# Eight smallest experts in two shared tiles of four instead of four shared tiles of two, with weights loaded in the order in which they are used

## The chip, the cores and the metric

The kernel runs on one core of one Trainium2 chip. The metric is device time in microseconds (us) of one launch. Three runs of the kernel before took 1531.68, 1537.52 and 1541.69 us; the median is 1537.52 us.

The engines are named as the profile names them: PE multiplies matrices (PEld is its weight load), DVE, ACT and POOL work on vectors, SP issues transfers. A line number such as L1372 is a line of the kernel before, unless the text says that it is of the changed kernel.

## The reference

One layer of a model on a sequence of 1024 tokens of 1024 values: a recurrent mixer with two branches, then a mixture of 32 experts in 4 groups of 8. The change touches only the mixture. What it computes:

```python
def hier_moe(h, w_rg, b_rg, w_re, b_re, w1e, w3e, w2e):
    t = h.reshape(-1, d)
    pg_top, g_idx = lax.top_k(softmax(t @ w_rg + b_rg), 1)          # one group of 4
    le_sel = (t @ w_re + b_re) of that group                        # its 8 experts
    pe_top, e_idx = lax.top_k(softmax(le_sel), TOP_K)               # TOP_K = 2
    wts = pg_top * pe_top / sum(pe_top)
    ...
    for e in range(N_EXPERTS):                                      # 32
        he = silu(t @ w1e[e]) * (t @ w3e[e])                        # 1024 -> 256
        out = out + cw[:, e:e + 1] * (he @ w2e[e])                  # 256 -> 1024
```

Each token is worked on by two experts, so there are 2048 rows of expert work in all. How many rows an expert gets comes from the data. With the reference's own inputs experts 0, 1 and 2 get 55, 19 and 15 rows, and the other 29, sorted by size, get 249, 197, 179, 137, 127, 88, 73, 73, 66, 64, 64, 61, 57, 53, 52, 51, 49, 47, 47, 38, 37, 29, 27, 22, 21, 16, 13, 11 and 11.

## The kernel before

The program is fixed when it is built, but which expert is large is known only on the chip. So there are **places**: experts 0 to 2 have places of their own (NF = 3) with 128 rows each, and the other 29 experts are sorted by size on the chip and take 29 places with a fixed number of rows, the classes CLS: 256, 224, 192 twice, 128 three times, 112, 96 three times, 80 twice and 64 sixteen times. A place of up to 128 rows is one tile of 128 partitions; a larger one is two tiles. Rows that do not fit into their place go to overflow tiles (NX = 16), which are worked on at the end, only where there are any. Two places of 64 rows are a **pair** and share one tile: partitions 0 to 63 hold the rows of the one, 64 to 127 those of the other.

The routing stage builds, for every tile, the list of the rows that belong on its partitions. 32 small matmuls (L1242) add up 0/1 matrices into `pi`, one column for each tile; the second member of a pair must land on partitions 64 to 127, so 32 more matmuls (L1245) with 64 columns add it there. Three DVE instructions make from `pi` the lists `sidx` (where a row of the result goes, L1249) and `gidx` (which token to fetch, L1250).

The expert stage is a list of **jobs**, one for each tile, worked on in order, each with its gather of 128 rows (POOL, L1289), transposes (PE, `turn` L1302, `turn2` L1362), `up` (1024 to 512 columns), `hidden` (L1324 to L1328), `down` (256 to 1024) and a scatter of the result (POOL, L1333). While a job's `up` runs the next job's rows are gathered, and its transposes stand behind that `up` on PE. The classes are interleaved: each class's units are spread evenly over the sequence. The jobs of the stage are, in order (S for a place of its own with its rows, x2 for two tiles, P for a pair):

```
before: S128 S128 S128 P S128 S96 P S192x2 S80 P P S256x2 S224x2 S128 S112 S96 P P S192x2 S80 P S128 S96 P
after:  S128 S128 S128 P S128 S96 S192x2 S80 Q P S256x2 S224x2 S128 S112 S96 P S192x2 S80 Q S128 S96 P
```

A single's weights are split into two parts that PE can multiply fast (`split`, ACT L1282 and DVE or POOL L1283, into 8 buffers each for `wh` and `wl`), and `up` and `down` do three such products for each step (L1315 to L1317, L1350 to L1352). A pair's weights are used as they are loaded, with one slower product for each step, and the two members' products go to different columns of PE's array (`up2` L1372, `down2` L1386):

```python
def up2(W, tp):
    ph = psum.tile([128, 512], F32, name="ph", bufs=2)
    for k in range(8):
        o = (k % 2) * 512
        for s_ in range(2):
            C = slice(64 * s_, 64 * s_ + 64)
            T.matmul(ph[C], tp[:, k, C], W[s_][k // 2][:, o:o + 512], start=(k == 0), stop=(k == 7))
```

An expert's weights are 6 **pieces** of 512 KB, c0 to c3 for `up` and c4 and c5 for `down`. All 192 pieces go through SP's one queue in a fixed order (L953) into NRAW = 16 buffers `w`; a piece's transfer waits until the piece 16 places before it has been used up, by its split (a single) or by PE (a pair). `issue` keeps the loads LA = 3 experts ahead in the program; what holds them back on the chip is the 16 buffers. Before the change the order is expert by expert, c0 to c5.

Of the kernel before, what the change touches and what calls it, by code (L numbers as in the profile page):

```python
# [21 lines left out]
LA = 3  # L22
# [70 lines left out]
def _build(tc, A, out, dump, stop, top):  # L93
    nc = tc.nc
    V, S, T, P, Y = nc.vector, nc.scalar, nc.tensor, nc.gpsimd, nc.sync
# [15 lines left out]
    psum = front.enter_context(pool("psum", 1, PSUM))  # L111
# [16 lines left out]
    ident = const.tile([128, 128], F32, name="ident")  # L128
# [61 lines left out]
    def derive(name, n):  # L190
# [5 lines left out]
                    op0=OP.mult, op1=OP.add)  # L196
# [521 lines left out]
    order = [(p, hf) for p in range(4) for hf in range(2)]  # L718
# [55 lines left out]
    psum = p3.enter_context(pool("psum3", 1, PSUM))  # L774
# [115 lines left out]
    iot = rpc.tile([128, 128], F32, name="iot")  # L890
# [18 lines left out]
    for d in range(8):  # L909
        merge(1, d)  # L910
        for kk in (2 * d, 2 * d + 1):
# [4 lines left out]
            h, l = (lambda t: (t[:, 0], t[:, 1]))(wo.tile([128, 2, 512], F32R, name="w", bufs=NRAW))  # L916
# [5 lines left out]
    if stop == "merged":  # L922
# [11 lines left out]
    NS = ND - 2 * NP  # L934
    NB = sum(c > 128 for c in CAP)

    NTP = NF + NB + NS
    NT0 = NTP + NP
    NT = NT0 + NX

    units = [[(p,) for p in range(sum(m for m, _ in CLS[:q]), sum(m for m, _ in CLS[:q + 1]))]
             for q in range(len(CLS) - 1)] + [[(NS + 2 * i, NS + 2 * i + 1) for i in range(NP)]]
    order = [p for _, u in sorted(((i + 0.5) / len(us), u) for us in units for i, u in enumerate(us)) for p in u]
    raws, src = {}, {}
    issued = [0]

# [9 lines left out]
    def issue(n):  # L956

        while issued[0] < min(n, 192):
            e, c = divmod(issued[0], 6)
            if c == 0:  # L960
# [57 lines left out]
    PO = [rp.tile([128, 2, 8, 128], BF, name=f"PO{i}") for i in range(2)]  # L1018
# [41 lines left out]
    with pool("xt", 1) as xt:  # L1060
# [78 lines left out]
    dmp("m_gt2", mrow["gt2"])  # L1139
    gidx = x1p.tile([128, NT], I32, name="gidx")  # L1140
    sidx = x1p.tile([128, NT], I32, name="sidx")
    ordi = x1p.tile([128, 32 + NX + 1], I32, name="ordi")
    with pool("psumr", 1, PSUM) as psum, pool("ro", 1, side="right") as ro:
        f = lambda shape, name, dt=F32, pl=rp: pl.tile(shape, dt, name=name)
# [8 lines left out]

        plan = f([32, 3, 32], "plan")
        for dst, base, step in ((plan[:, 0, 0:NB], NF, 2), (plan[:, 0, NB:NS], NF + 2 * NB, 1),
                                (plan[:, 0, NS:ND:2], NTP, 1), (plan[:, 0, NS + 1:ND:2], NT, 1),
                                (plan[:, 0, ND:32], 0, 1)):
# [32 lines left out]
        c = lambda i: cc[:, i:i + 1]  # L1190
# [37 lines left out]
        ts = f([128, 2, 8], "ts")  # L1228
# [7 lines left out]
        RT = f([128, 2, 8, NT + NP], "RT", BF, pl=ro)  # L1236
        bt = lambda ap: ap.to_broadcast([128, 2, 8, NT + NP])
        last = V.tensor_tensor(RT, bt(iot[:, None, None, 0:NT + NP]), bt(ts[:, :, :, None]), op=OP.is_equal)
        pi = psum.tile([128, NT], F32, name="pi")
        ajh = [(a, j, h) for a in range(2) for j in range(8) for h in range(2)]  # L1240
        for a, j, h in ajh:
            T.matmul(pi, PO[h][:, a, j], RT[:, a, j, 0:NT], start=((a, j, h) == ajh[0]), stop=False,  # L1242
                     skip_group_check=True)
        for a, j, h in ajh:
            T.matmul(pi[64:128, NTP:NT0], PO[h][:, a, j, 0:64], RT[:, a, j, NT:], start=False,  # L1245
                     stop=((a, j, h) == ajh[-1]), skip_group_check=True)
        li = f([128, NT], "li", pl=ro)
        V.tensor_scalar(li, pi, 0.0, 4096.0, op0=OP.is_equal, op1=OP.mult)
        V.scalar_tensor_tensor(sidx, pi, -1.0, li, op0=OP.add, op1=OP.add)  # L1249
        V.tensor_scalar(gidx, sidx, 1, None, op0=OP.arith_shift_right)  # L1250
# [23 lines left out]
    with pool("psume", 1, PSUM) as psum, pool("ew", 1) as ew, pool("ex", 2) as ex:  # L1274
# [19 lines left out]
        def turn(xg, m):  # L1294

            R = slice(0, m)
            th = ex.tile([128, 8, 128], F32R, name="th")
            tl = ex.tile([128, 8, 128], F32R, name="tl")
            for i in range(2):
                pt = psum.tile([128, 4, 128], F32, name="pt", bufs=3)  # L1300
                for k in range(4):
                    T.transpose(pt[:, k, R], xg[R, (4 * i + k) * 128:(4 * i + k) * 128 + 128], ident[R, R])  # L1302
# [51 lines left out]
            scatter(yt, ti, m)  # L1354


        def turn2(xg):
            tp = ex.tile([128, 8, 128], F32, name="th")
            for i in range(2):
                pt = psum.tile([128, 4, 128], F32, name="pt", bufs=3)  # L1360
                for k in range(4):
                    T.transpose(pt[:, k], xg[:, (4 * i + k) * 128:(4 * i + k) * 128 + 128], ident)  # L1362
                S.copy(tp[:, 4 * i:4 * i + 4], pt)  # L1363
            return tp

        def up2(W, tp):
            ph = psum.tile([128, 512], F32, name="ph", bufs=2)
            for k in range(8):
                o = (k % 2) * 512
                for s_ in range(2):  # L1370
                    C = slice(64 * s_, 64 * s_ + 64)
                    T.matmul(ph[C], tp[:, k, C], W[s_][k // 2][:, o:o + 512], start=(k == 0), stop=(k == 7))  # L1372
            return ph

        def down2(W, ph, ti):
            pt = hidden(ph, 128)
            ep = ex.tile([128, 2, 128], F32, name="eh")
            S.copy(ep, pt[:, 0:2])
            yt = ex.tile([128, 1024], F32, name="yt")
            for hf in range(2):  # L1380
                sl = slice(hf * 512, hf * 512 + 512)
                py_ = psum.tile([128, 512], F32, name="py", bufs=3)
                for k in range(2):
                    for s_ in range(2):
                        C = slice(64 * s_, 64 * s_ + 64)
                        T.matmul(py_[C], ep[:, k, C], W[s_][4 + k][:, sl], start=(k == 0), stop=(k == 1))  # L1386
# [3 lines left out]
        def tiles_of(p):  # L1390
            b = NF + p + min(p, NB)
            return [(b + i, min(128, CAP[p] - 128 * i)) for i in range(-(-CAP[p] // 128))]


        jobs = [((e,), e, 128) for e in range(NF)]
        for n, p in enumerate(order):
            if p < NS:
                jobs += [((NF + n,), t, m) for t, m in tiles_of(p)]
            elif (p - NS) % 2 == 0:
                jobs.append(((NF + n, NF + n + 1), NTP + (p - NS) // 2, 128))  # L1400
# [12 lines left out]

        def turned_of(n, xg):
            es, _, m = jobs[n]
            return turn2(xg) if len(es) == 2 else turn(xg, m)
# [4 lines left out]
        for n, (es, ti, m) in enumerate(jobs):  # L1421
            nxt = jobs[n + 1] if n + 1 < len(jobs) else None
            if nxt:
                xg = gather(n + 1, *nxt[1:])
            pair = len(es) == 2
# [68 lines left out]
```

## Time and profile before

| | |
|---|---|
| median of three runs | 1537.52 us |
| profiled execution | 1536.43 us |
| its span, first to last instruction | 1534.5 us |
| PE busy | 1326.4 us (86%), mean granted clock 0.945 |
| DVE, ACT, POOL busy | 920.1, 490.3, 408.1 us |
| expert stage: first transposes to last `down` on PE | 1137.1 to 1466.6 us |
| jobs in it: tiles of singles, pairs | 20, 8 |
| last piece of weights issued by SP | 1442.5 us |

How to read it: in the profile times are in us from the first instruction and "mean ns" is that of one instruction. PE's matmuls overlap, so the distance between starts tells what one costs, not its length. A slow product is two matmul instructions in the trace. A stage is judged by what its last engine waits for: PE for weights, or SP's queue for a buffer that PE still holds. "DMA share" is the part of the time in which the 16 transfer engines were busy, and GB/s what they moved.

### The profile page before, as it was taken

To read this page: it belongs to the slowest core of one execution; us is meant where nothing else is said; L and a number is where in the kernel's file an instruction comes from. 1 tells how busy PE (TensorE), PEld (TensorE's weight loads), DVE (VectorE), ACT (ScalarE), POOL (GpSimd) and SP (SyncE) were. 2 spreads that over 40 slices of the span, in tenths; PEclk is the share of its full clock that TensorE was granted. 3 is DMA by queue.
4 is the path that set the end of the run, shared out by engine and by line. 5 is a ranking of instruction groups with operands and counts; after the bars stand their busy time and mean duration, and the time that the engine had idled before them with its cause. 6 is when DMAs were issued, how large, how long until landed. Compare 5 with 4: busy or idle time off the path is not lost.

```text
span 1534.5 us, 23186 instructions
## 1 busy us (share of the span) xinstructions
PE 1326.4 (86%) x8524; PEld 926.5 (60%) x8524; DVE 920.1 (60%) x2073; ACT 490.3 (32%) x900; POOL 408.1 (27%) x327
## 2 busy tenths in 40 slices
PE   1898998899999999999999797899759899999910
PEld 0686765666766667766766475687545555755500
DVE  8936868687658562475433577614775435625557
ACT  3222323132222222231211693312424424514321
POOL 7001212121101110111111326601314434634514
PEclk9998999999999999999999899999969999999965
DMA  6333432333433211112211754541448979979952
GB/s 262 130 117 138 126 110 92 99 99 115 151 131 94 66 57 35 51 57 60 63 42 35 238 167 150 187 163 56 165 165 299 385 281 402 349 267 393 349 234 100
DMA packets 113403, 248.59 MB, mean 162 GB/s; under 512 B 39632, under 2 KB 40960, under 8 KB 112256
## 3 DMA queue, kind: packets, MB, share of 16 engines
q1 hardware_dynamic: 105952, 230.22, 42.7%
q0 software_dynamic: 7328, 16.79, 3.0%
q8 instruction: 69, 1.13, 0.3%
q14 instruction: 54, 0.44, 0.1%
HBM read 218.16 MB, written 38.36 MB: 167 GB/s over the span
## 4 chain that ended last, share of the span: by engine, by line
PE 60%; DVE 20%; DMA 9%; ACT 4%; issue 4%; POOL 2%; POOLq 0%; SPq 0%; DVEq 0%; ACTq 0%
PE pg L319 5%; PE pg L318 5%; PE pg L320 5%; DMA xg<-h2d,gidx 3%; DMA w<-in_we 3%; PE ph L1372 3%; PE pj L318 2%; DVE wa L228 2%; PE pj L320 2%; PE pj L319 2%; PE st L603 2%; PE ph L1315 2%; PE st L617 2%; PE pj L1106 2%; PE ph L1317 2%
## 5 line engine op out<-in xcount | busy, mean ns | idle before, releaser
L318 PE MATMUL pg<-hh,wh 128*128 128x512 f32 x376 | 158.9, 423 | 8.4 <-DVE cr L680 5.0
L319 PE MATMUL pg<-hl,wh 128*128 128x512 f32 x376 | 157.2, 418 | 0.0
L320 PE MATMUL pg<-hh,wl 128*128 128x512 f32 x376 | 155.9, 415 | 0.0
L560 POOL TENSOR_TENSOR WV<-VT,m 128x512 f32<-128x512 f32 x32 | 35.5, 1110 | 369.5 <-PE st L603 280.3
L1282 ACT CAST wh<-w 128x1024 fp32r<-128x1024 f32 x96 | 98.5, 1053 | 82.1 <-DMA w<-in_we 30.7
L1283 DVE TENSOR_TENSOR wl<-w,wh 128x1024 fp32r<-128x1024 f32 x68 | 92.0, 1376 | 36.1 <-ACT wh L1282 33.7
L228 DVE SCALAR_TENSOR_TENSOR wa<-wa,cb 128x1024 f32<-128x1024 f32 x64 | 79.6, 1251 | 27.1 <-DMA wa<-in_wada 27.0
L318 PEld LDWEIGHTS pg<-hh,wh 128*128 128x128 f32 x376 | 72.3, 192 | 33.3 <-issue 9.4
L216 ACT CAST wh<-wr 128x512 fp32r<-128x512 f32 x88 | 54.4, 619 | 100.0 <-PE pj L319 50.4
L217 DVE TENSOR_TENSOR wl<-wr,wh 128x512 fp32r<-128x512 f32 x72 | 53.5, 742 | 50.7 <-ACT wh L216 50.4
L319 PEld LDWEIGHTS pg<-hl,wh 128*128 128x128 f32 x376 | 72.3, 192 | 17.7 <-issue 4.7
L320 PEld LDWEIGHTS pg<-hh,wl 128*128 128x128 f32 x376 | 71.9, 191 | 17.2 <-issue 4.0
L610 DVE SCALAR_TENSOR_TENSOR St<-St,Dc,st 128x64 f32<-128x64 f32 x128 | 35.4, 277 | 76.4 <-PE st L608 76.3
L318 PE MATMUL pj<-hh,wh 128*128 128x512 f32 x192 | 77.5, 404 | 3.2 <-DVE carry L365 3.2
L1283 POOL TENSOR_TENSOR wl<-w,wh 128x1024 fp32r<-128x1024 f32 x28 | 71.0, 2541 | 30.6 <-ACT wh L1282 23.1
L320 PE MATMUL pj<-hh,wl 128*128 128x512 f32 x192 | 76.9, 401 | 0.0
L319 PE MATMUL pj<-hl,wh 128*128 128x512 f32 x192 | 75.8, 395 | 0.0
L1315 PE MATMUL ph<-wh,th 128*128 128x512 f32 (+4 forms) x160 | 65.4, 409 | 7.1 <-ACT th L1304 6.8
L515 DVE TENSOR_TENSOR X<-X,UC 128x60 f32<-128x60 f32 (+24 forms) x248 | 65.9, 266 | 4.2
L1372 PE MATMUL ph<-w,th 128*64 128x512 f32 x256 | 65.7, 598 | 1.8 <-ACT th L1363 1.7
L513 DVE TENSOR_TENSOR UC<-X,Ui 128x60 f32<-128x60 f32 (+24 forms) x248 | 63.3, 255 | 4.4
L1317 PE MATMUL ph<-wh,tl 128*128 128x512 f32 (+4 forms) x160 | 63.9, 399 | 1.9 <-DVE tl L1305 1.9
(503 smaller groups left out, 3139.0 us busy)
## 6 DMA issues: line engine op xcount, KB each, us to landing
w<-in_we SPq DMA_DIRECT2D x192, 512.0 KB
wa<-in_wada SPq DMA_DIRECT2D x64, 512.0 KB
wr<-in_win SPq DMA_DIRECT2D x72, 256.0 KB
gd<-gt SPq DMA_DIRECT2D x32, 256.0 KB
g<-gd SPq DMA_DIRECT2D x32, 256.0 KB
yy<-yd SPq DMA_DIRECT2D x8, 1024.0 KB
xT<-in_xT SPq DMA_DIRECT2D x8, 512.0 KB
Ui<-Ud SPq DMA_DIRECT2D x32, 128.0 KB
```

Source lines behind the costliest of these rows:

```text
L216: S.copy(h[:, :n], raw)
L228: V.scalar_tensor_tensor(wa, wa, 1.0, cb, op0=OP.mult, op1=OP.mult, accum_out=ccol[:, i:i + 1])
L318: T.matmul(ps, wh[:, o:o + 128], hh[k][:, sl], start=(k == 0), stop=False)
L319: T.matmul(ps, wh[:, o:o + 128], hl[k][:, sl], start=False, stop=False)
L320: T.matmul(ps, wl[:, o:o + 128], hh[k][:, sl], start=False, stop=(k == n - 1))
L513: V.tensor_mul(t_, X[:, :nj, s:s + 1].to_broadcast([128, nj, nt]), Ui[:, s, None, s + 1:32].to_broadcast([128, nj, nt]))
L515: V.tensor_add(X[:, :nj, s + 1:32], X[:, :nj, s + 1:32], t_)
L1282: S.copy(h, raw)
L1283: (P if pool_engine else V).tensor_sub(l, raw, h.bitcast(F32))
L1315: T.matmul(ph[R], th[:, k, R], h[:, o:o + 512], start=(k == 0), stop=False)
L1317: T.matmul(ph[R], tl[:, k, R], h[:, o:o + 512], start=False, stop=(k == 7))
L1372: T.matmul(ph[C], tp[:, k, C], W[s_][k // 2][:, o:o + 512], start=(k == 0), stop=(k == 7))
```

## The change

The 16 places of 64 rows become 8 places of 64 (4 pairs) and 8 places of 32, the smallest, in 2 tiles of four (Q, a **quad**): 26 jobs instead of 28. `up2` and `down2` loop over two or four members with 64 or 32 partitions each. The pieces of a shared tile are loaded c0 of every member, then c1 of every member, and so on. The sets of rows that a shared tile's later members need are no longer added by 32 matmuls: `pi` gets 10 extra columns, and after `sidx` and `gidx` of the single tiles are made, five small products with a shifted identity (`shf_`) move those columns to partitions 32, 64 or 96 and add them, and the lists of the shared tiles are made from that.

```diff
-    NF, NX, NP = 3, 16, 8
-    CLS = ((1, 256), (1, 224), (2, 192), (3, 128), (1, 112), (3, 96), (2, 80), (2 * NP, 64))
+    NF, NX, NP, NQ = 3, 16, 4, 2
+    CLS = ((1, 256), (1, 224), (2, 192), (3, 128), (1, 112), (3, 96), (2, 80), (2 * NP, 64), (4 * NQ, 32))
...
+    NG_ = NP + 3 * NQ
...
+    order, pieces, upto = [], [(e, c) for e in range(NF) for c in range(6)], {e: 6 * e + 6 for e in range(NF)}
+    for _, u in sorted(((i + 0.5) / len(us), u) for us in units for i, u in enumerate(us)):
+        es = tuple(NF + len(order) + q for q in range(len(u)))
+        order += u
+        pieces += [(e, c) for c in range(6) for e in es]
...
-            e, c = divmod(issued[0], 6)
+            e, c = pieces[issued[0]]
...
+        shf_ = f([64, 224], "shf_", pl=ro)
+        P.memset(shf_, 0.0)
+        P.tensor_copy(shf_[:, 96:160], ident[0:64, 0:64])
...
-            T.matmul(pi, PO[h][:, a, j], RT[:, a, j, 0:NT], start=((a, j, h) == ajh[0]), stop=False,
+            T.matmul(pi, PO[h][:, a, j], RT[:, a, j], start=((a, j, h) == ajh[0]), stop=((a, j, h) == ajh[-1]),
                      skip_group_check=True)
-        for a, j, h in ajh:
-            T.matmul(pi[64:128, NTP:NT0], PO[h][:, a, j, 0:64], RT[:, a, j, NT:], start=False,
-                     stop=((a, j, h) == ajh[-1]), skip_group_check=True)
...
+        lists(0, NTP, pi[:, 0:NTP])
+        gh = f([128, NT + NG_ - NTP], "gh", pl=ro)
+        V.tensor_copy(gh, pi[:, NTP:])
+        ps_ = psum.tile([128, NT - NTP], F32, name="ps_")
+        g0 = NT - NTP
+        T.matmul(ps_, ident, gh[:, 0:g0], start=True, stop=False, skip_group_check=True)
+        T.matmul(ps_[:, 0:NP], shf_[0:64, 32:160], gh[0:64, g0:g0 + NP], start=False, stop=False,
+                 skip_group_check=True)
+        for q in range(1, 4):
+            T.matmul(ps_[:, NP:NP + NQ], shf_[0:32, 96 - 32 * q:224 - 32 * q],
+                     gh[0:32, g0 + NP + (q - 1) * NQ:g0 + NP + q * NQ], start=False, stop=(q == 3),
+                     skip_group_check=True)
+        lists(NTP, NT, ps_)
...
+        def parts(W):
+            w = 128 // len(W)
+            return [(i, slice(w * i, w * i + w)) for i in range(len(W))]
...
-                for s_ in range(2):
-                    C = slice(64 * s_, 64 * s_ + 64)
+                for s_, C in parts(W):
                     T.matmul(ph[C], tp[:, k, C], W[s_][k // 2][:, o:o + 512], start=(k == 0), stop=(k == 7))
...
-                issue(6 * (es[-1] + 1 + LA))
+                issue(max(upto[es[-1]] + 6 * LA, upto[nxt[0][-1]]))
```

What PE works through where the third and fourth pair stood, before. `pt<-ident,xg` are the transposes of the next job's rows, `pt<-ident,he` those of `hidden`; `ph<-w,th` is `up2` and `py<-w,eh` is `down2`, each row with the size of its result and xN for N alike in a row:

```order
L1372 MATMUL ph<-w,th 64x512 x15
L1362 MATMUL pt<-ident,xg_10157 128x128 x8
L1328 MATMUL pt<-ident,he 128x128 x2
L1372 MATMUL ph<-w,th 64x512
L1386 MATMUL py<-w,eh 64x512 x8
L1372 MATMUL ph<-w,th 64x512 x15
L1302 MATMUL pt<-ident,xg_10156 128x128 x8
L1328 MATMUL pt<-ident,he 128x128 x2
```

And after, with the line numbers of the changed kernel (`up2` is L1421, `down2` L1434), from the first quad's `up` to the `up` of the pair that follows it:

```order
L1421 MATMUL ph<-w,th 32x512 x31
L1408 MATMUL pt<-ident,xg_10144 128x128 x8
L1373 MATMUL pt<-ident,he 128x128 x2
L1347 MATMUL pt<-ident,xg_10145 128x128 x6
L1434 MATMUL py<-w,eh 32x512 x8
L1347 MATMUL pt<-ident,xg_10145 128x128 x2
L1434 MATMUL py<-w,eh 32x512 x8
L1421 MATMUL ph<-w,th 64x512 x16
```

Before, a pair's `up` is 16 products of 64 result rows; a quad's is 32 of 32 result rows (one more stands ahead of the rows shown). Behind the quad's `up` stand the transposes of two further jobs, then the quad's `down` in two halves, and only behind it the next pair's `up`.

The second place is DVE at the end of the routing stage, where the first lists are made, between the splits `wl` of the first expert's weights. Before:

```order
L1248 TENSOR_SCALAR li<-pi 128x44
L1263 TENSOR_REDUCE ef<-eo 128x16
L1249 SCALAR_TENSOR_TENSOR sidx<-pi,li 128x44
L1264 TENSOR_SCALAR ef<-ef 128x16
L1283 TENSOR_TENSOR wl<-w,wh 128x1024
L1250 TENSOR_SCALAR gidx<-sidx 128x44
```

And after:

```order
L1278 TENSOR_SCALAR li<-pi 128x20
L1308 TENSOR_REDUCE ef<-eo 128x16
L1279 SCALAR_TENSOR_TENSOR sidx<-pi,li 128x20
L1285 COPY gh<-pi 128x32
L1280 TENSOR_SCALAR gidx<-sidx 128x20
L1309 TENSOR_SCALAR ef<-ef 128x16
L1328 TENSOR_TENSOR wl<-w,wh 128x1024
```

`gidx`, which the first gather needs, now stands ahead of a split instead of behind it; the lists of the shared tiles follow later, between further splits.

More of the change, by code (lines that the diff above doesn't have):

```diff
@@ L923, in _build, with tiles_of @@
         raise Stop
-    NF, NX, NP = 3, 16, 8
-    CLS = ((1, 256), (1, 224), (2, 192), (3, 128), (1, 112), (3, 96), (2, 80), (2 * NP, 64))
+    NF, NX, NP, NQ = 3, 16, 4, 2
+    CLS = ((1, 256), (1, 224), (2, 192), (3, 128), (1, 112), (3, 96), (2, 80), (2 * NP, 64), (4 * NQ, 32))
     CAP = [c for n, c in CLS for _ in range(n)]
     ND = 32 - NF
-    NS = ND - 2 * NP
+    NS = ND - 2 * NP - 4 * NQ
     NB = sum(c > 128 for c in CAP)
     NTP = NF + NB + NS
-    NT0 = NTP + NP
+    NTQ = NTP + NP
+    NT0 = NTQ + NQ
     NT = NT0 + NX
+    NG_ = NP + 3 * NQ
+    def tiles_of(p):
+        b = NF + p + min(p, NB)
+        return [(b + i, min(128, CAP[p] - 128 * i)) for i in range(-(-CAP[p] // 128))]
     units = [[(p,) for p in range(sum(m for m, _ in CLS[:q]), sum(m for m, _ in CLS[:q + 1]))]
-             for q in range(len(CLS) - 1)] + [[(NS + 2 * i, NS + 2 * i + 1) for i in range(NP)]]
-    order = [p for _, u in sorted(((i + 0.5) / len(us), u) for us in units for i, u in enumerate(us)) for p in u]
+             for q in range(len(CLS) - 2)]
+    units += [[(NS + 2 * i, NS + 2 * i + 1) for i in range(NP)],
+              [tuple(NS + 2 * NP + 4 * i + q for q in range(4)) for i in range(NQ)]]
+    jobs = [((e,), e, 128) for e in range(NF)]
+    order, pieces, upto = [], [(e, c) for e in range(NF) for c in range(6)], {e: 6 * e + 6 for e in range(NF)}
[3 more added lines that the diff above has]
+        pieces += [(e, c) for c in range(6) for e in es]
+        for e in es:
+            upto[e] = len(pieces)
+        if len(u) == 1:
+            jobs += [(es, t, m) for t, m in tiles_of(u[0])]
+        elif len(u) == 2:
+            jobs.append((es, NTP + (u[0] - NS) // 2, 128))
+        else:
+            jobs.append((es, NTQ + (u[0] - NS - 2 * NP) // 4, 128))
     raws, src = {}, {}
@@ L958, in issue @@
         while issued[0] < min(n, 192):
-            e, c = divmod(issued[0], 6)
-            if c == 0:
+            e, c = pieces[issued[0]]
+            if e not in src:
                 src[e] = A["we"][e] if e < NF else chosen(order[e - NF])
@@ L1155, in _build @@
         for dst, base, step in ((plan[:, 0, 0:NB], NF, 2), (plan[:, 0, NB:NS], NF + 2 * NB, 1),
-                                (plan[:, 0, NS:ND:2], NTP, 1), (plan[:, 0, NS + 1:ND:2], NT, 1),
+                                (plan[:, 0, NS:NS + 2 * NP:2], NTP, 1),
+                                (plan[:, 0, NS + 1:NS + 2 * NP:2], NT, 1),
+                                (plan[:, 0, NS + 2 * NP:ND:4], NTQ, 1),
+                                *((plan[:, 0, NS + 2 * NP + q:ND:4], NT + NP + (q - 1) * NQ, 1)
+                                  for q in range(1, 4)),
                                 (plan[:, 0, ND:32], 0, 1)):
@@ L1235, in _build @@
         V.tensor_add(ts, ts, tf)
[L1236 to L1239, printed above, removed]
+        RT = f([128, 2, 8, NT + NG_], "RT", BF, pl=ro)
+        bt = lambda ap: ap.to_broadcast([128, 2, 8, NT + NG_])
+        last = V.tensor_tensor(RT, bt(iot[:, None, None, 0:NT + NG_]), bt(ts[:, :, :, None]), op=OP.is_equal)
@@ L1240, in _build @@
+        pi = psum.tile([128, NT + NG_], F32, name="pi")
         ajh = [(a, j, h) for a in range(2) for j in range(8) for h in range(2)]
         for a, j, h in ajh:
[L1242 removed]
+            T.matmul(pi, PO[h][:, a, j], RT[:, a, j], start=((a, j, h) == ajh[0]), stop=((a, j, h) == ajh[-1]),
                      skip_group_check=True)
[L1244 to L1246 removed]
@@ L1247, in _build, with lists @@
         li = f([128, NT], "li", pl=ro)
-        V.tensor_scalar(li, pi, 0.0, 4096.0, op0=OP.is_equal, op1=OP.mult)
-        V.scalar_tensor_tensor(sidx, pi, -1.0, li, op0=OP.add, op1=OP.add)
-        V.tensor_scalar(gidx, sidx, 1, None, op0=OP.arith_shift_right)
+        def lists(c0, c1, pi):
+            V.tensor_scalar(li[:, c0:c1], pi, 0.0, 4096.0, op0=OP.is_equal, op1=OP.mult)
+            V.scalar_tensor_tensor(sidx[:, c0:c1], pi, -1.0, li[:, c0:c1], op0=OP.add, op1=OP.add)
+            V.tensor_scalar(gidx[:, c0:c1], sidx[:, c0:c1], 1, None, op0=OP.arith_shift_right)
@@ L1383, in down2 @@
                 for k in range(2):
-                    for s_ in range(2):
-                        C = slice(64 * s_, 64 * s_ + 64)
+                    for s_, C in parts(W):
                         T.matmul(py_[C], ep[:, k, C], W[s_][4 + k][:, sl], start=(k == 0), stop=(k == 1))
@@ L1388, in down2 @@
             scatter(yt, ti, 128)
[L1390 to L1400, printed above, removed]
         W = {}
@@ L1415, in turned_of @@
             es, _, m = jobs[n]
[L1416 removed]
+            return turn2(xg) if len(es) > 1 else turn(xg, m)
         issue(6 * LA)
@@ L1424, in _build @@
                 xg = gather(n + 1, *nxt[1:])
-            pair = len(es) == 2
+            pair = len(es) > 1
             ph = up2([W[e] for e in es], tt.pop(n)) if pair else up(W[es[0]], tt.pop(n), m)
```

## The prediction

> **What bounds the kernel now.** The change acts from about 1112 us of the span on, in the routing lists and the expert stage. I read the slices of the page first, then the stage cut into windows, then PE's order of time, then what SP's queue waits for.
>
> ```profile
> PE   1898998899999999999999797899759899999910
> DMA  6333432333433211112211754541448979979952
> core 0: us, PE busy (x) PEld busy (x) DVE busy (x) ACT busy (x) POOL busy (x), PEclk, DMA share, GB/s
> 1137.00:1467.00 330.00, 306.75 (x1384) 186.58 (x1384) 160.29 (x205) 134.32 (x201) 138.82 (x81) 0.98 0.88 326
> 1186.00:1467.00 281.00, 262.49 (x1195) 156.25 (x1194) 132.10 (x172) 107.17 (x165) 118.92 (x70) 0.99 0.89 336
> 1370.00:1415.00 45.00, 43.34 (x207) 26.07 (x206) 21.25 (x28) 18.02 (x29) 19.38 (x12) 1.00 1.03 401
> 1250.00:1265.00 15.00, 14.95 (x68) 6.86 (x66) 2.12 (x4) 1.66 (x4) 1.95 (x2) 1.00 0.54 173
> 1293.00:1297.00 4.00, 3.83 (x18) 3.00 (x17) 2.03 (x5) 0.37 (x1) 0.24 (x1) 1.00 1.04 414
> ```
>
> In the expert stage (slices 30 to 38) both PE and the transfers are nearly full: PE 93% and DMA 88% of 330 us. They take turns. In 1250 to 1265 PE is full and the transfers half empty, at 173 GB/s; where they are full they move 401 GB/s over 45 us, and 414 at the best. The stage moved 330 x 0.326 = 107.6 MB, which at 401 GB/s takes 268 us. So transfers alone would need 268 us and PE 307: PE sets the pace, with a reserve of weights behind it that is thin.
>
> ```profile
> 1205.27 1.03 PE L1362 MATMUL pt<-ident,xg 128*128 128x128 f32 x8
> 1219.91 1.09 PE L1302 MATMUL pt<-ident,xg 128*128 128x128 f32 x8
> 1258.22 7.08 PE L1372 MATMUL ph<-w,th 128*64 128x512 f32 x30
> 1265.23 1.09 PE L1362 MATMUL pt<-ident,xg 128*128 128x128 f32 x8
> 1267.34 3.77 PE L1386 MATMUL py<-w,eh 128*64 128x512 f32 x16
> 1270.82 7.03 PE L1372 MATMUL ph<-w,th 128*64 128x512 f32 x30
> 1277.78 1.09 PE L1302 MATMUL pt<-ident,xg 128*128 128x128 f32 x8
> 1289.61 0.39 PE L1317 MATMUL ph<-wh,tl 128*128 128x512 f32 x1
> 1370.54 1.09 PE L1362 MATMUL pt<-ident,xg 128*128 128x128 f32 x8
> 1383.09 1.09 PE L1302 MATMUL pt<-ident,xg 128*128 128x128 f32 x8
> 1419.84 7.08 PE L1372 MATMUL ph<-w,th 128*64 128x512 f32 x30
> 1462.98 3.65 PE L1386 MATMUL py<-w,eh 128*64 128x512 f32 x16 [0.46 <-ACT eh L1378]
> ```
>
> These are rows of PE's timeline. From the transposes at 1265.23 to those at 1277.78 PE works through one pair: 12.55 us, and 1370.54 to 1383.09 is 12.55 again. The pair at 1205.27 took 14.64, since it waited for weights. The last `down` ends at 1466.63.
>
> ```profile
> SPq L953 <- DMA w<-in_we: 62.9, 65, 5.1
> SPq L953 <- PE ph L1372: 42.6, 26, 14.3
> 1440.86 1.61 SPq L953 DMA_DIRECT2D w<-in_we  x2
> w<-in_we SPq DMA_DIRECT2D x192, 512.0 KB
> ```
>
> SP's queue waits 42.6 us, once for 14.3, for a buffer that a pair's `up` on PE still holds: those are the holes in the transfers. The last of 192 pieces is issued at 1442.5, and PE works on for 24 us. Weights are not late at the end; PE is.
>
> **The change part by part.** *Two jobs fewer.* 28 jobs become 26, and the work inside a quad is the same as in a pair if four column groups run at once as two do. PE then saves 2 x 12.55 = 25.1 us. The pieces stay 192 and the token rows 2048, so the transfers save nothing.
>
> *The quad's own products.* A quad issues 64 matmuls in `up` and 32 in `down`, a pair 32 and 16.
>
> ```profile
> L1372 PE MATMUL ph<-w,th 128*64 128x512 f32 x256 | 65.7, 598 | 1.8 <-ACT th L1363 1.7
> L493 PE MATMUL aq<-AR,BT 64*32 64x32 f32 x512 | 6.3, 199 | 1.8 <-DVE BT L474 1.8
> ```
>
> A pair's matmul lasts 598 ns, but 30 of them end in 7.08 us: (7.08 - 0.59) / 15 = 0.43 us for two side by side. No quad stands in the trace. The nearest row is L493, an earlier stage, whose products also have 32 columns and go to four column groups (and two row groups): 512 x 199 ns = 102 us of matmuls lie in 6.3 us, 16 at once. So the ends are 7.1 + 3.7 = 10.7 us for a quad's products (four at once) and 96 x 0.43 = 41.3 us (one at a time). I take 10.7, the end that L493 is near to. Against it: the Trainium skill, TensorE: Matmul & The Clock Gate, Part 3, gives 3.07 times for four packed groups, not 4; no run here shows that. An estimate by that page is 10.7 x 4 / 3.07 = 13.9 us; weights that come later still would hide most of it, and the sum would be about 1 us higher.
>
> *The first quad.* A quad needs 24 pieces and there are 16 buffers: its `up` pieces c0 to c3 fill all of them. Its c4 and c5 can only be issued when PE has used c0, and behind them in SP's queue stand the next pair's and the next single's pieces. So from that moment on the transfers run without holes and PE waits for them. PE gets there earlier by the pair that stood at 1205.27, 14.64 us: `up` starts at 1258.22 - 14.64 = 1243.6, and c0, the first two of eight steps, is done a quarter of 7.08 later, 1245.3. Until the first 256-row tile has its c3, 8 + 12 + 4 = 24 pieces of 0.524 MB must come, and about 450 token rows of 4 KB: 12.6 + 1.8 = 14.4 MB, at 401 GB/s 36.0 us. I add 2 us until they flow again (an estimate; the ends are 0 and the 7.7 us from the first gather's issue to the transposes that use it). That is 1283.3.
>
> ```profile
> L1282 ACT CAST wh<-w 128x1024 fp32r<-128x1024 f32 x88 | 90.5, 1054 | 82.1 <-DMA w<-in_we 30.7 <-PE ph L1317 27.6 <-PE pt L1362 9.4
> L1283 DVE TENSOR_TENSOR wl<-w,wh 128x1024 fp32r<-128x1024 f32 x60 | 82.6, 1397 | 36.1 <-ACT wh L1282 33.7 <-DMA w<-in_we 1.5
> ```
>
> Its split takes 1.05 + 1.40, and the last six matmuls at 0.23 (three fill 0.68 us in PE's timeline) 1.4: `up` ends at 1287.2, where it ended at 1289.61 + 0.39 = 1290.0 before. Of 14.64 us 2.8 are left. PE's new order puts 11 matmuls of the second 256-row tile in between, 2.5 us of work done while waiting: 5.3.
>
> *Up to the second quad.* From there to the next pair seven tiles of singles follow, as before; PE sets their pace and 5.3 stays. Two pairs ended at 1383.09, now one: 5.3 + 12.55 = 17.9.
>
> *The second quad and the end.* Its `up` starts at 1419.84 - 17.9 = 1401.9 and gives c0 back at 1403.6. All 32 remaining pieces, 16.8 MB, and some 260 rows, 1.1 MB, come after that: 17.9 MB, 44.6 us, plus 2: the last piece lands at 1450.2. Ten of the last `down`'s 16 matmuls are left then, 3.65 x 10 / 16 = 2.3: 1452.5 against 1466.63, **14.1 us** saved.
>
> *The clock.* PE now waits several us behind each quad.
>
> ```profile
> 1346.82 0.64 PE L1328 MATMUL pt<-ident,he 112*128 112x112 f32 x2 [3.11 <-DVE he L1325]
> 1348.00:1353.00 5.00, 5.00 (x13) 3.65 (x13) 0.96 (x2) 0.00 (x0) 1.75 (x1) 0.50 1.02 400
> ```
>
> After a wait of 3.11 us the granted clock was 0.50, and 13 matmuls took 5.0 us where 13 x 0.23 = 3.0 would do. I charge 3 us, for two quads and the last `down`; the ends are 0 and 6.
>
> *The routing.*
>
> ```profile
> L1245 PE MATMUL pi<-RT,PO 128*64 128x8 bf16 x32 | 1.9, 195 | 0.0
> L1242 PE MATMUL pi<-RT,PO 128*128 128x44 bf16 x32 | 1.3, 208 | 5.5 <-DVE RT L1238 5.5
> 1127.20 1.22 DVE L1283 TENSOR_TENSOR wl<-w,wh 128x1024 fp32r<-128x1024 f32 x1
> 1128.34 0.18 DVE L1250 TENSOR_SCALAR gidx<-sidx 128x44 int32<-128x44 int32 x1
> 1129.40 1.44 POOL L1289 DMA_INDIRECT xg<-h2d,gidx  x1 [19.89 <-DVE ordi L1266]
> ```
>
> 32 matmuls, 1.9 us, go; 44 columns become 52, at most 1.3 x 8 / 44 = 0.2. `gidx` no longer stands behind a split of 1.22, and one copy stands ahead of it: it comes about 1 us earlier. The first experts' later splits are pushed back by four small DVE instructions of 0.2, some 0.7. The five small products fall into PE's wait for the first rows, and POOL's memset and copy into its 19.89 us of idle time. The first jobs also wait for weights that are split by DVE. I take 0, between -1 and +0.7.
>
> **Sum.** 1536.43 - 14.1 + 3 = 1525.3. The profiled execution is 1.1 below the median of 1537.52, so I say **1525.5**, 0.8% below the median.
>
> **The rivals.** *Most of the saving stays* (1515.7). The whole 25.1 (1511.3) would need the first 14.4 MB in about 24 us, 600 GB/s, and no row shows more than 414. With 414, no 2 us of start and no clock loss, the two waits shrink by 3.2 and 3.4 us: 14.1 + 6.6 = 20.7 saved. For it: pieces that come without holes are what 414 was measured on.
>
> *The weights eat it all* (1535 to 1541). With the stage's mean, 336 GB/s, the two waits grow by 6.9 and 8.7 us: 14.1 - 15.6 - 3 is a loss of 4.5. For it: 65 waits of SP for earlier pieces to land. Against it: 336 contains the holes. The Trainium skill, DMA: Bandwidth & Descriptors, Where 436 GB/s comes from, says that about 358 GB/s binds a transfer from memory to a core; the 401 over 45 us speaks against that here. By 358 the waits grow by 4.2 and 5.4, and the time is 1535.
>
> *Slower*: PE does not run four column groups of 32 at once. One at a time a quad's products take 41.3 instead of 10.7 us, 61 us for two: 1536.43 - 25.1 + 61.2 = 1572.5. It decides from 10.7 + 12.55 = 23.3 us of products on, where a quad costs more than the two pairs that it replaces; two at a time (21.4) is still no loss. Against it is the row of L493.
>
> *It doesn't do what it says*: an expert with over 32 rows on a small place would go to an overflow tile, at least 18 us each (7.8 to load 3.1 MB, 2.5 split, 36 x 0.23 products). The eight smallest have 29 to 11 rows, so there is none.
>
> **How the numbers follow.** Chances: the forecast 0.60, most of the saving stays 0.22, the weights eat it 0.13, slower 0.05. A measurement of this kernel can tell about 1% (15 us) from no change. Faster by over 1% means below 1522.1, which only the first rival gives: 0.22. Within 1%: 0.60 + 0.13 = 0.73. Slower: 0.05. The range takes in the first rival with 2 us more, and the second to its middle: 1514 to 1538.
>
> **What would show it.** A quad's `up` of about 7 us and `down` of about 3.7 without its wait (right), or 14 and more (wrong). Behind each quad a wait of PE for `w`, 5 us or more, and DMA shares near 1 at 400 GB/s for some 40 us. In the long stretch ahead of each quad SP waiting for PE. The first 256-row `up` ending near 1287, the last `down` near 1453 to 1456, 2 to 5 us after the last piece, where it was over 16 before. `gidx` near 1127.4. I am wrong if transfers stay below 380 GB/s behind the quads, if PE reaches the first quad later than 1246, or if another engine's order (ACT's casts of singles behind a quad's copies) holds PE longer than the weights do.

## The result, and the profile after

| | before | after |
|---|---|---|
| median, twelve runs each | 1535.82 us | 1527.93 us |
| ratio, 95% interval | | 0.9942 (0.9924 to 0.9959) |
| profiled execution, its span | 1536.43, 1534.5 us | 1529.99, 1528.2 us |
| first transposes to last `down` on PE | 1137.1 to 1466.6: 329.6 us | 1137.0 to 1459.9: 322.9 us |

The changed kernel is 0.6% faster: 8.9 us by the ratio, 7.9 between the medians; 12 were forecast. The two profiled executions differ by 6.4 us, and their expert stages by 6.7.

The slices of the page, and windows over the stage and over the stretch behind each quad's first products (start and end, length, busy us of each engine with its instructions, granted clock, DMA share, GB/s):

```profile
PE   0999899899999999999999798899848998989810
DMA  6334432323442211112210654442358979978962
1137.00:1467.00 330.00, 293.48 (x1364) 172.82 (x1364) 157.22 (x201) 131.39 (x193) 136.32 (x78) 0.98 0.89 330
1241.00:1245.00 4.00, 4.00 (x44) 1.17 (x36) 0.00 (x0) 0.00 (x0) 0.95 (x1) 1.00 0.65 185
1241.10:1282.40 41.30, 34.62 (x164) 10.50 (x156) 7.01 (x11) 7.81 (x14) 5.36 (x6) 1.00 0.98 377
1246.00:1292.00 46.00, 38.52 (x158) 16.04 (x152) 14.16 (x16) 12.67 (x20) 11.10 (x7) 1.00 1.02 394
1410.00:1455.00 45.00, 39.54 (x172) 19.51 (x166) 18.89 (x24) 17.82 (x25) 14.84 (x8) 1.00 1.01 404
```

PE is busy 293 us of the stage where it was 307: less work. Behind each quad the transfers now run full for 45 us, at 394 and 404 GB/s, and PE idles beside them with the clock at 1.00.

PE's timeline around the first quad, from the transposes of its rows to those of the first 224-row tile (start, length, instruction, and in brackets what it waited for):

```profile
1234.68 1.04 PE L1408 MATMUL pt<-ident,xg 128*128 128x128 f32 x8
1239.98 7.07 PE L1421 MATMUL ph<-w,th 128*32 128x512 f32 x62
...
1252.97 1.90 PE L1434 MATMUL py<-w,eh 128*32 128x512 f32 x10 [1.17 <-DMA w<-in_we]
1254.80 0.44 PE L1347 MATMUL pt<-ident,xg 128*128 128x128 f32 x2
1255.17 6.19 PE L1434 MATMUL py<-w,eh 128*32 128x512 f32 x16
...
1263.30 2.35 PE L1421 MATMUL ph<-w,th 128*64 128x512 f32 x8 [0.93 <-DMA w<-in_we]
...
1269.47 2.48 PE L1421 MATMUL ph<-w,th 128*64 128x512 f32 x8 [1.26 <-DMA w<-in_we]
...
1282.86 0.50 PE L1361 MATMUL ph<-wl,th 128*128 128x512 f32 x1 [1.88 <-DVE wl L1328]
...
1297.03 1.03 PE L1347 MATMUL pt<-ident,xg 128*128 128x128 f32 x8
```

and the rows of before at the same three places, the transposes ahead of the pairs where the quads now stand and those of the first 224-row tile:

```profile
1252.89 1.03 PE L1362 MATMUL pt<-ident,xg 128*128 128x128 f32 x8
...
1301.24 1.03 PE L1302 MATMUL pt<-ident,xg 128*128 128x128 f32 x8
...
1414.51 1.04 PE L1362 MATMUL pt<-ident,xg 128*128 128x128 f32 x8
```

PE reaches the first quad 1252.89 - 1234.68 = 18.2 us earlier, and the 224-row tile only 4.2 earlier: **14.0 us are lost behind the first quad.** The brackets show only a few of these. The rest hides in rows that read as busy: 16 product instructions of `down2` take 6.19 us here, where all 32 of a quad take 3.64 when their pieces are there (half_loads, below). The page counts a product that has started as busy, and products that follow their pieces one by one no longer overlap. So a stretch is to be compared with the same stretch, not by its idle time.

The second quad and the end:

```profile
1398.48 1.03 PE L1408 MATMUL pt<-ident,xg 128*128 128x128 f32 x8
1403.77 7.07 PE L1421 MATMUL ph<-w,th 128*32 128x512 f32 x62
...
1424.24 0.50 PE L1361 MATMUL ph<-wl,th 128*128 128x512 f32 x1 [0.93 <-DVE wl L1328]
...
1456.23 3.70 PE L1434 MATMUL py<-w,eh 128*64 128x512 f32 x16 [0.46 <-ACT eh L1427]
```

16.0 us ahead at the quad, 6.7 at the end (1459.93 against 1466.63): **9.3 us are lost behind the second quad.** What SP's queue waits for from 1186 us on (in total, times, longest), and its row where the first quad gives its first buffers back and so opens the gate for the transfers that stand behind:

```profile
SPq L976 <- DMA w<-in_we: 74.8, 76, 2.8
SPq L976 <- PE ph L1421: 26.0, 12, 10.1
1241.11 2.01 SPq L976 DMA_DIRECT2D w<-in_we  x2
```

The queue stands for 10.1 us on a buffer that a quad's `up` holds; it goes on at 1241.1, 1.1 us after that `up`'s main part began.

### The profile page after: what moved, and what is told of

Its sections match the earlier page's. It is cut to its first block, busy times and chain, and to the rows that moved or that the text cites. A ratio compares the mean times of both kernels' runs of the same rounds, so it can differ in the third digit from the quotient of the medians.

```text
span 1528.2 us, 23082 instructions
## 1 busy us (share of the span) xinstructions
PE 1321.9 (87%) x8482; PEld 919.1 (60%) x8482; DVE 917.9 (60%) x2071; ACT 487.0 (32%) x892; POOL 402.5 (26%) x331
## 4 chain that ended last, share of the span: by engine, by line
PE 58%; DVE 19%; DMA 12%; ACT 4%; issue 4%; POOL 3%; SPq 0%; POOLq 0%; DVEq 0%; ACTq 0%
DMA w<-in_we 9%; PE pg L318 6%; PE pg L319 6%; PE pg L320 6%; PE pj L318 3%; PE pj L320 2%; PE pj L319 2%; PE st L603 2%; DVE wa L228 2%; PE st L617 2%; PE pj L1129 2%; PE pj L1128 2%; PE pj L1127 2%; PE ph L1421 2%; PE ph L1360 1%
## 5 line engine op out<-in xcount | busy, mean ns | idle before, releaser
L318 PEld LDWEIGHTS pg<-hh,wh 128*128 128x128 f32 x376 | 73.0, 194 | 33.3 <-issue 12.5
L1328 POOL TENSOR_TENSOR wl<-w,wh 128x1024 fp32r<-128x1024 f32 x28 | 68.6, 2455 | 19.0 <-ACT wh L1327 12.5
L1378 POOL DMA_INDIRECT yd<-yt,sidx x26 | 41.7, 1606 | 99.8 <-DVE yt L1435 41.6
L1361 PE MATMUL ph<-wl,th 128*128 128x512 f32 (+4 forms) x160 | 64.2, 401 | 4.0 <-DVE wl L1328 3.9
```

Of the source, the lines that this page charges most:

```text
L318: T.matmul(ps, wh[:, o:o + 128], hh[k][:, sl], start=(k == 0), stop=False)
L1328: (P if pool_engine else V).tensor_sub(l, raw, h.bitcast(F32))
L1361: T.matmul(ph[R], th[:, k, R], l[:, o:o + 512], start=False, stop=False)
```

## The experiments

The profiles were read by stretches, since the executions differ ahead of the stage: its first transposes come between 1128.2 and 1140.7 us. *Stretch 1* runs from the transposes of the first quad's rows to those of the first 224-row tile (it holds the quad, a pair and both 256-row tiles, in any order, but for the `down` of the last of them, which stands behind those transposes), *stretch 2* from the transposes of the second quad's rows to the end of the last `down`.

| | median us | ratio to before, interval | stretch 1 | stretch 2 |
|---|---|---|---|---|
| the change | 1527.93 | 0.9942 (0.9924 to 0.9959) | 62.3 | 61.4 |
| lists_only | 1535.09 | 0.9997 (0.9978 to 1.0017) | | |
| pairs_by_use | 1535.31 | 0.9989 (0.9967 to 1.001) | | |
| half_loads | 1505.40 | 0.9781 (0.9749 to 0.9813) | 48.3 | 55.7 |
| pair_later | 1519.85 | 0.9876 (0.984 to 0.9911) | 55.6 | 61.7 |
| early_up | 1524.34 | 0.99 (0.9873 to 0.9926) | 59.1 | 59.8 |
| early_later | 1517.91 | 0.9865 (0.9838 to 0.9892) | 51.9 | 59.0 |
| early_all | 1516.96 | 0.9867 (0.9831 to 0.9903) | 51.6 | 61.6 |
| nw6 | 1534.86 | 0.9974 (0.9955 to 0.9993) | 60.2 | 61.5 |
| four_more | 1528.64 | 0.9922 (0.9892 to 0.9952) | 56.7 | 58.4 |
| early_four | 1520.29 | 0.9891 (0.986 to 0.9922) | 50.8 | 59.4 |
| last_six_fewer | 1524.52 | 0.9919 (0.9891 to 0.9947) | 61.4 | 61.1 |
| members_apart | 1554.53 (one run) | | | |

Of each edit the lines that matter are shown, and `...` stands for lines left out.

**Which part of the change acts.** Two runs keep eight pairs:

```diff
 # lists_only
-    NF, NX, NP, NQ = 3, 16, 4, 2
+    NF, NX, NP, NQ = 3, 16, 8, 0
...
-        pieces += [(e, c) for c in range(6) for e in es]
+        pieces += [(e, c) for e in es for c in range(6)]
...
```

> The changed kernel with eight pairs and no quad, and with the pieces expert by expert as before: of the change only the routing lists are left. Theory (the lists cost nothing, weights and PE's jobs are everything): the time of the kernel before, ratio 0.998 to 1.002. Rival (the lists brought a part of the 0.6%): ratio 0.995 or less; if they cost, 1.003 or more.

> As lists_only, but with the new order of pieces (c0 of both members, then c1 of both). Theory: a pair's 12 pieces fit into 16 buffers and are there before PE comes, so the order alone changes nothing: ratio 0.997 to 1.002. Rival (loading in order of use is what brought the gain): ratio 0.995 or less, with lists_only at 1.

pairs_by_use has the first of these two edits only. Ratios 0.9997 and 0.9989, both with 1 in the interval: neither the lists nor, for pairs, the order of the pieces does anything that these runs can tell (0.2%, some 3 us). The gain is the quads'. Quads with their pieces expert by expert were not run by themselves, so what the order is worth to a quad is not shown.

**What the quads are worth without late weights.**

```diff
-        pieces += [(e, c) for c in range(6) for e in es]
+        pieces += [(e, c) for c in range(6) for e in es[:2]]
...
-                    W[e] = [raws.pop((e, c)) for c in range(6)]
+                    W[e] = [raws.pop((e, c)) for c in range(6)] if (e, 0) in raws else W[e - 2]
```

> The changed kernel, but a quad loads the weights of its first two members only and its members 3 and 4 are multiplied with the same tiles: the same products on PE, 24 pieces fewer. Theory (the quads save 25 us on PE, and the late weights take back 14 to 18 of it): the waits behind the quads go, ratio 0.982 to 0.986, some 25 us below the kernel before and 15 below the changed one. Rival (the quad's products, the clock or the casts hold PE): the ratio stays at 0.992 to 0.996.

The ratio is 0.9781, beyond the forecast. The stage takes 302.7 us (1133.6 to 1436.3), 26.9 less than before, near the 25 forecast; the 31 us between the medians hold some 4 more that the stage does not show. PE's timeline from the transposes ahead of the first quad to those of the 224-row tile:

```profile
1231.52 1.04 PE L1408 MATMUL pt<-ident,xg 128*128 128x128 f32 x8
...
1246.24 3.64 PE L1434 MATMUL py<-w,eh 128*32 128x512 f32 x32
1249.81 7.08 PE L1421 MATMUL ph<-w,th 128*64 128x512 f32 x30
...
1279.80 1.04 PE L1347 MATMUL pt<-ident,xg 128*128 128x128 f32 x8
```

The quad's whole `down` takes 3.64 us, and the pair's `up` follows at once. Stretch 1 is 48.3 us without a wait for weights, so 62.3 - 48.3 = 14.0 us of waits were in it, the same number as above by another way. So the rivals (the quad's products, the casts, the clock) fall there: with the same products and fewer pieces the time is gone.

Stretch 2, 55.7 us in half_loads, is not free of waits. At its start:

```profile
1383.15 0.36 PE L1373 MATMUL pt<-ident,he 80*128 80x80 f32 x2 [1.50 <-DVE he L1370]
1384.69 1.05 PE L1421 MATMUL ph<-w,th 128*32 128x512 f32 x2 [1.19 <-ACT th L1409]
1385.70:1388.70 3.00, 3.00 (x8) 1.81 (x8) 0.14 (x1) 0.57 (x1) 3.00 (x2) 0.50 0.82 243
1390.15 7.07 PE L1421 MATMUL ph<-w,th 128*32 128x512 f32 x62
```

PE waits for `he` and `th`, ahead of which DVE and ACT have work on the weights of a later single (`wl` at 1381.55, `wh` at 1383.11), and behind these waits the granted clock is 0.50 for 3 us (the third row, a window). The prediction had named another engine's order and the clock as dangers; in the change neither is seen at this place. So the second quad is better compared from its main products on: to the end of the stage half_loads takes 1436.3 - 1390.2 = 46.1 us, before (a pair) 1466.6 - 1419.8 = 46.8, and the change 1459.9 - 1403.8 = 56.1. The loss of 9.3 us behind the second quad comes out again.

**What follows the quad.** The 19 units behind the first three experts, by their number in the order:

```diff
...
+    seq_ = [u for _, u in sorted(((i + 0.5) / len(us), u) for us in units for i, u in enumerate(us))]
+    for u in [seq_[i] for i in [0, 1, 2, 3, 4, 5, 7, 6, 8, 9, 10, 11, 12, 13, 14, 15, 16, 17, 18]]:
```

> The changed kernel with one place in the order of jobs exchanged: the pair that follows the first quad goes behind the 256-row single, so that the quad is followed by two tiles that need 6 pieces in all, not by a pair that needs 12. Nothing else. Theory (PE runs out of weights because the pieces of the quad and of what follows it come in one queue behind the quad's start): about 4.5 us less than the changed kernel, ratio 0.990 to 0.993, and PE waits less than half as long behind the first quad. Rival (the whole stage's bytes set the end): the time of the changed kernel, 0.994 to 0.996.

The ratio is 0.9876, and its interval lies wholly below that of the change. PE's timeline:

```profile
1235.84 1.04 PE L1409 MATMUL pt<-ident,xg 128*128 128x128 f32 x8
...
1260.93 1.92 PE L1435 MATMUL py<-w,eh 128*32 128x512 f32 x8
1263.09 0.73 PE L1361 MATMUL ph<-wh,th 128*128 128x512 f32 x2 [0.24 <-ACT wh L1328]
1265.39 0.50 PE L1362 MATMUL ph<-wl,th 128*128 128x512 f32 x1 [1.57 <-DVE wl L1329]
...
1284.38 7.08 PE L1422 MATMUL ph<-w,th 128*64 128x512 f32 x30
1291.39 1.09 PE L1348 MATMUL pt<-ident,xg 128*128 128x128 f32 x8
```

The stretch takes 55.6 us where it took 62.3. Of these 6.7 us 0.6 come from its end, which here leaves out the `down` of the pair and not that of the single: up to the transposes of the second 224-row tile, behind both, it is 66.9 us and was 73.0. So 6.1 us of the 14.0 lost behind the first quad are won back. While PE works on two tiles that share 6 pieces, the pair's 12 come, and its `up` of 7.08 us runs through. Stretch 2, which the edit leaves alone, stays at 61.7. About 6 us are seen in the stretch where 4.5 were expected; the medians, 1527.93 and 1519.85 in two series of runs, differ by 8.

**When the gate opens.**

```diff
...
                 tt[n + 1] = turned_of(n + 1, xg)
+                if len(nxt[0]) == 4:
+                    issue(max(upto[es[-1]] + 6 * LA, upto[nxt[0][-1]]))
+                    begin(nxt[0])
+                    phs[n + 1] = up2([W[e] for e in nxt[0]], tt.pop(n + 1))
```

> The changed kernel with the same order of jobs and pieces, but a quad's up stands on PE ahead of the down of the job before it, not behind it. Theory (the 16 buffers that the quad's c0 to c3 fill are the gate for all that follows): the gate opens 3 us earlier for each quad, and the down of 3 us is done while c4 and c5 come; 5 to 6 us less than the changed kernel, ratio 0.989 to 0.992. Rival (transfers run at their limit over the whole stage and only their sum counts): no change, 0.993 to 0.996.

> early_up and pair_later together. Theory: both act on the same waits but on different parts of them, so the gains add up for the second quad and nearly so for the first: 9 to 12 us less than the changed kernel, ratio 0.985 to 0.989. Rival (one of them already took all that was to be had): no better than pair_later, 0.988.

The ratio 0.99 of early_up is below 0.9942, but the intervals overlap a little. The stretches carry it: 3.2 and 1.6 us shorter, 4.8 together, a little under the 5 to 6 expected. With pair_later together, stretch 1 is 51.9, only some 4 above that without waits. The ratio 0.9865 is what was expected, though the intervals of early_later and pair_later overlap, so time alone doesn't tell these two apart.

```diff
-                if len(nxt[0]) == 4:
+                if len(nxt[0]) > 1:
```

> early_later, and a pair's up too stands ahead of the down of the job before it. Theory (PE waits only behind quads; a pair's 12 pieces fit into the buffers): nothing to gain, the time of early_later within 2 us, ratio 0.985 to 0.988. Rival (every earlier release of a buffer fills a hole in the transfers, and the next wait shrinks): 3 us or more less, 0.984 or below.

0.9867 against 0.9865: a pair's `up` has nothing to gain. (Its stretch 2, 61.6 against 59.0, is longer in the one execution profiled. Most of that, 2.4 us, lies where the last pair's `up` now stands among the products of the `down` before it; why these take longer together is open.)

**The number of buffers.** nw6 has the first line of this edit alone, four_more all of it, and early_four all of it on top of early_later:

```diff
-NW = 8
+NW = 6
+NQX = 4
...
-            raws[e, c] = load(src[e], c)
+            own = xq[0] is not None and c == 4 and e in quads
+            raws[e, c] = load(src[e], c, xq[0].tile([128, 1024], F32, name="wq", bufs=NQX) if own else None)
...
```

> The changed kernel with four raw buffers more, used only for the c4 pieces of the quads, and, to make room, 6 split buffers instead of 8. To be compared with nw6. Theory (what stops the transfers ahead of a quad is that its c0 to c3 fill all 16 buffers): four pieces come before the quad starts, so everything behind it comes 4 x 1.3 = 5 us earlier; over both quads 6 to 10 us less than nw6. Rival (the rate of the transfers alone): the time of nw6.

> The changed kernel with 6 split buffers instead of 8 and nothing else: the control for four_more. Theory: a single's six splits still fit, and where PE waits it is for pieces: within 3 us of the changed kernel, ratio 0.993 to 0.997. Rival (splits made ahead of PE are part of the reserve): slower by 5 us or more, 0.998 and above.

> early_later with four_more's four buffers for the quads' c4 and its 6 split buffers. Theory: what is left of the waits behind the quads shrinks by up to 5 us each, and 6 split buffers cost some 3.6 us as nw6 showed against the changed kernel: 0 to 6 us less than early_later, ratio 0.983 to 0.987. Rival (the waits are gone already and only the cost of the split buffers stays): 3 to 4 us more than early_later, 0.988 to 0.990.

four_more against nw6 is 0.9922 to 0.9974, 6.2 us by the medians, and both stretches are 3 us shorter: buffers, not only the rate, hold the transfers back. nw6 lies between its theories. Its time behind the quads is no longer than that of the change, but from the first transposes to the first quad it takes 1241.8 - 1137.6 = 104.2 us against 97.7. So six split buffers cost 6.5 us there, all ahead of the first quad: splits made in advance are a reserve. In early_four that price (104.0 us where early_later has 98.2) outweighs the rest: 0.9891, no better than early_later, as its rival had it, though its stretch 1 is the shortest of all kernels that load every piece.

**What sets the end.** The last pair's second member uses its first member's weights:

```diff
-        pieces += [(e, c) for c in range(6) for e in es]
+        pieces += [(e, c) for c in range(6) for e in (es[:1] if 31 in es else es)]
...
-                    W[e] = [raws.pop((e, c)) for c in range(6)]
+                    W[e] = [raws.pop((e, c)) for c in range(6)] if (e, 0) in raws else W[e - 1]
```

> The changed kernel, but the last pair loads the weights of its first member only and its second member is multiplied with the same tiles: the same products, and the last 6 of the 192 pieces do not come. It asks what sets the end behind the second quad. The prediction's step (the last piece lands, and 2.3 us later PE is done): the end comes earlier by up to 6 x 1.3 = 7.8 us, until PE's own work stops it, ratio 0.989 to 0.991. Theory now (PE waits only until the first single behind the quad has its weights, and from there works 35 us at its own pace, with the pieces ahead of it): within 2 us of the changed kernel, ratio 0.993 to 0.996.

The ratio, 0.9919 (0.9891 to 0.9947), reaches into both forecasts. The trace decides:

```profile
1392.58 1.04 PE L1408 MATMUL pt<-ident,xg 128*128 128x128 f32 x8
...
1450.05 3.65 PE L1434 MATMUL py<-w,eh 128*64 128x512 f32 x16 [0.46 <-ACT eh L1427]
```

Stretch 2 is 1453.7 - 1392.6 = 61.1 us, with all pieces 61.4. The last pieces do not set the end.

**Four column groups side by side.**

```diff
-        pieces += [(e, c) for c in range(6) for e in es]
+        pieces += [(e, c) for e in es for c in range(6)]
...
-            for k in range(8):
-                o = (k % 2) * 512
-                for s_, C in parts(W):
+            for s_, C in parts(W):
+                for k in range(8):
+                    o = (k % 2) * 512
```

> The changed kernel with up's products of a shared tile written member by member (all eight steps of one, then of the next), so that neighbours on PE go to the same column group, and the pieces expert by expert to match. The down keeps its order. Theory: four column groups run side by side only if their products stand next to each other; alone a product instruction costs 0.43 us, so a quad's up takes 64 x 0.43 = 27.5 us where it took 6.9, and a pair's 32 x 0.43 = 13.8 where it took 7.1; 2 x 20.6 + 4 x 6.7 = 68 us of PE's time more, of which the waits behind the quads (15 us) hide a part: 50 to 70 us above the changed kernel. Rival (PE overlaps them whatever their order): the products' lengths stay and the time is within 10 us of the changed kernel.

A quad's `up` and `down` on PE, and the group of all its `down` products, first of this kernel, then that group in the changed kernel:

```profile
1414.73 16.56 PE L1421 MATMUL ph<-w,th 128*32 128x512 f32 x46
1432.23 7.05 PE L1421 MATMUL ph<-w,th 128*32 128x512 f32 x16
1441.12 3.64 PE L1434 MATMUL py<-w,eh 128*32 128x512 f32 x32
L1434 PE MATMUL py<-w,eh 128*32 128x512 f32 x64 | 7.3, 595 | 0.0
```

```profile
L1434 PE MATMUL py<-w,eh 128*32 128x512 f32 x64 | 18.7, 601 | 2.5 <-DMA w<-in_we 1.9 <-ACT eh L1427 0.6
```

16 product instructions of one member take 7.05 us, (7.05 - 0.59) / 15 = 0.43 each; in the changed kernel 62 of them, side by side, fit into 7.07. So here products overlap only where neighbours in the program go to different column groups. The 46 instructions in 16.56 us are a little quicker than 0.43 each, since at a change of member four of them run beside the last four of the member before. The time, 1554.5, is only 27 us above the change, not 50 to 70: the stage is 352.4 us, 29.5 longer. That the slower products hide much of what had been waiting behind the quads fits this, but the order of the pieces was changed too, and this one run does not part the two. The second group row shows the waits from the other side: the same 64 product instructions of `down2` are "busy" 7.3 us here and 18.7 in the changed kernel, 11 us of waiting that no idle time shows.

## Why the prediction was right, step by step

The forecast was 1525.5 us, 12 below the three runs' median; 8.9 by the ratio (0.58% of 1536) came, 7.9 by the medians. Its mechanism holds: two jobs fewer on PE, and weights that come too late behind each quad take most of that back. Three of its terms were off, and two of the errors offset each other, which was luck.

- *Two jobs fewer, 25.1 us.* Right: without late weights the stage is 26.9 shorter (half_loads). The prediction counted 14.64 us for the pair ahead of the first quad; PE was there 18.2 earlier, since some 2.5 us that had been lost behind that pair went with it, and another 1 us had been gained at the first pair.
- *The quad's products, 10.7 us.* Right: 7.07 for 62 of 64 products of `up`, all 64 in 7.07 in early_up's profile, and 3.64 for `down`. 64 x 0.43 / 7.07 is a gain of 3.9 times. The Trainium skill, TensorE: Matmul & The Clock Gate, Part 3, has 3.07 times for four row groups, the figure that was weighed, and 2.38 for three column groups; what this trace shows for four column groups is higher. The rival that PE takes them one at a time is out.
- *The wait behind the first quad, 14.64 - 5.3 = 9.3 us.* The mechanism is right and the size wrong: 14.0. Two terms were too small. The first is the transfers. The gate opened at 1241.1, not 1245.3, but c3 of the first 256-row single was there only at 1282.37 (where its cast begins, below), almost the 1283.3 that were forecast: 41.3 us and not 38, so that all that PE was earlier than forecast was lost. The 2 us of start were right: 185 GB/s over the first 4 us is 2.2 us lost against 401. So was the rate, 394 in the window behind it. But from the gate to 1282.4 the window has 41.3 us x 377 GB/s = 15.6 MB, 1.2 more than the 24 pieces and 450 rows, which is 3 us; that parts of later pieces and results on their way out move at the same time is likely, but the rows don't divide them. The second is the split. From c3 to the end of `up` 1.05 + 1.40 + 1.4 = 3.9 us were reckoned; it took 7.5, to 1289.9 (ACT's `he` starts on the result at 1289.94), where `up` had ended at 1290.0 before. DVE comes to this single's four splits only at 1281.60, behind two `yt` of the pair, and the last ends at 1288.43. PE was not idle then: from 1282.86 to the transposes of the 224-row tile it worked on both 256-row tiles, with a single wait of 0.3 us, and what it did of the second one in advance is the 4.2 us that were left.

```profile
1281.60 6.83 DVE L1328 TENSOR_TENSOR wl<-w,wh 128x1024 fp32r<-128x1024 f32 x4
1282.37 1.05 ACT L1327 CAST wh<-w 128x1024 fp32r<-128x1024 f32 x1 [0.24 <-DMA w<-in_we]
1289.94 0.39 ACT L1369 ACTIVATE he<-ph 128x256 f32<-128x256 f32 x1 [2.34 <-PE ph L1362]
```

- *The second quad and the end, 17.9 - 14.1 = 3.8 us.* Here the step itself was wrong. It let the last piece set the end, 2.3 us ahead of it. That piece came at 1453.9, not 1450.2 (by the semaphore that its transfer raises in the trace), and PE worked on for 6.0 us. Before it had come at 1454.1, 12.5 us ahead of the end; the reserve of 24 us was counted from its issue. last_six_fewer shows that it doesn't set the end: without the last six pieces nothing changes. What does is PE's own chain behind the first single: this gets its second kind of product only at 1424.24, and two singles and a pair take 35.7 us more, to 1459.93. In half_loads the same products take 32.9 (from 1403.39 to 1436.26), so even here some 3 us are still waits. The loss was 9.3.
- *The clock, 3 us,* cost nothing: 1.00 in both windows behind the quads. The single waits there stay under 2 us in the brackets; the row of before with 0.50 had followed one of 3.11. So 3 us were charged for something that did not come, and they made up for half of the 5.5 that the step above was short. In the sum, 1525.3 + 1.1 would have been 1526.4; 1525.5 leaves most of that 1.1 out.
- *The routing, 0.* Right by lists_only, within the 3 us that it can tell. The list of the first rows is ready at 1129.99, not 1127.4, but that execution was 3.1 us later already ahead of the lists (the row `cc<-pn,cst` of DVE: 1112.03 before, 1115.12 after), so the list itself comes 1.4 us earlier than before, where 1 was forecast. The first transposes stand at 1137.03, as before.

```profile
1129.99 0.18 DVE L1280 TENSOR_SCALAR gidx<-sidx 128x20 int32<-128x20 int32 x1
1137.03 1.94 PE L1347 MATMUL pt<-ident,xg 128*128 128x128 f32 x8 [4.43 <-DMA xg<-h2d,gidx]
```

- *The rivals.* The weights ate 23.3 us in all (14.0 + 9.3), so "most of the saving stays" failed, and they left 6.7 of the 30.0 that PE had gained (18.2 up to the first quad, 11.8 up to the second), so "the weights eat it all" failed too. The page that would have given the latter, the Trainium skill, DMA: Bandwidth & Descriptors, Where 436 GB/s comes from, has 358 GB/s as what binds; 394 over 46 us and 404 over 45 us speak against it for one core alone.

## What to carry to other kernels

When work is packed more densely on the engine that sets the pace, ask what each job needs from the next slower resource while it runs: a quad is some 12 us of PE and 24 pieces, 31 us of transfers, and the average of the stage hides that. With a fixed number of buffers a job that fills them all holds up every transfer behind it until it starts; what stands behind it in the order matters as much as its own cost, and moving one pair behind the quad won nearly as much again as the change itself (5.4 us of the stage against 6.7). And compare a stretch with the same stretch of a kernel without the wait, since matmuls that follow their operands one by one read as busy.

The best version run was early_later (early_all the same within its interval): 1517.9 us, ratio 0.9865 (0.9838 to 0.9892), faster than both kernels.

## What the runs showed of the hardware that was not expected

- A product instruction with 32 result columns costs 0.43 us when it stands alone, as much as two side by side with 64 each in a pair of before; in these runs overlap comes only from neighbours in other column groups, four instructions deep at a change of group.
- The profiled executions differ by up to 12.5 us in where the stage begins (1128.2 to 1140.7), though the programs are nearly alike up to there, while stretch 2 of the change, pair_later, nw6 and last_six_fewer, whose edits lie elsewhere or do nothing there, agrees within 0.6 us (61.1 to 61.7). A few us are read better from a stretch than from one execution's total.
